# Decoder trunk on one core: FFN openings of four columns side by side, and x issued from ScalarE's queue

## The chip, the cores and the metric

The kernel runs on one core of a Trainium2 chip. The metric is the device time of one execution in microseconds (us); the time of a kernel is the median of several executions.

## The reference

Two layers work on a residual `h` of 256 positions by 1024 features in float32. Each layer has an FFN, a mixer and a second FFN; layer 0's mixer is attention (two head groups), layer 1's a Mamba-2 block.

```
for layer in range(2):
    h = h + 0.5 * swiglu(rmsnorm(h, ffn1_norm[layer]), w_gate, w_up, w_down)
    h = h + mixer(rmsnorm(h, mix_norm[layer]))
    h = h + 0.5 * swiglu(rmsnorm(h, ffn2_norm[layer]), w_gate, w_up, w_down)

swiglu(x) = (silu(x @ w_gate) * (x @ w_up)) @ w_down     # 1024 -> 2816 -> 1024
rmsnorm(x, g) = x * rsqrt(mean(x * x) + eps) * g
```

So there are four FFNs. The change concerns how each of them begins, and how the first one gets its data.

## The kernel before, in words

**Layout.** `h` lies transposed in SBUF: 8 tiles (`KT` = 8, index k) of 128 features by 256 positions. All products are made from split operands: a float32 number is cut into a high part and a low rest, and a product is high x high + high x low + low x high. `refresh(k)` (lines 202 to 210) makes the two halves of input tile k: ScalarE scales `h` by the gain into the high half of `xhl` (L205), VectorE computes the low half (L206). `squares(k)` (L212 to L216) squares `h` on ScalarE (L214) and adds up on POOL into `sqa` (L216).

**Weights.** All weights stream through class `Weights` in the order of use, as units of 128 x 1024 numbers (512 KB). SyncE's queue loads a unit into one of 4 `raw` buffers (L71); ScalarE rounds it to the high part `hi` (L86, a cast), VectorE subtracts for the low part `lo` (L87), into one of 8 pairs of buffers. `take()` (L91) hands out a unit and queues the conversion of units up to 4 ahead. The first unit is converted in four parts of 256 columns, the second in two of 512, all others whole.

**An FFN.** `ffn` (L356) makes 22 gate columns and 22 up columns of 128 outputs each (index f), then 8 down columns. A column is 8 *pieces*, one for each k; a piece (L338) is two matmuls, L339 (`hi` against both halves of the input, 512 wide) and L340 (`lo` against the high half, 256 wide). Both halves of a sum land in one PSUM bank. `total` (L360) copies the right half out on ScalarE (L363) and adds it on VectorE (L365). `gate` multiplies by the norm factor `rB` (L370), applies Silu (L371) and multiplies again (L372); `up` multiplies the two sums (L377) and splits the result into `ht` (L184, L185). In the first f the gate column and the up column run up to k = 6, and both get their k = 7 after that.

**The norm.** The norm factor of a row isn't put into the input: it is multiplied onto the sums afterwards. So the matmuls of a stage can begin before the norm is known. `norm_job` (L218) is a job in two steps among the matmuls: step one sums `sqa` over partitions on TensorE (L223), VectorE adds eps (L227), POOL takes the power -1/2 (L228); step two spreads the result over partitions on TensorE (L233) and ScalarE copies it to SBUF as `rB` (L237).

**What sets the order.** Each piece advances a clock of the program by 0.35 (`tick`, L341); a posted job makes its next step when the clock passes its due time. `post_norm` (L241) posts the norm with a delay of `L_N0` = 6.5, and its second step comes `L_N1` = 3.0 later. `need(nj)` (L384) makes whatever steps are left at once; it stands at the end of f = 0, after 16 pieces. A scheduler then orders each engine's instructions; `high_priority` moves instructions forward. Within an engine, instructions run in that order.

**The start of the program.** SyncE issues the gains `gn`, then parts of the input x and of weight unit 0 in turn (L130, L136), then the next units. TensorE has six matmuls on an identity matrix as a warm-up (L855; each of these float32 matmuls shows as two in the profile). `refresh` runs for k = 0 to 7 with the conversions of three units between, and then the squares.

PSUM has 8 banks: four in pool `mm` (`bank()`), two in `sb` (`sbank()`, used by the mixers alone) and two in `tp` (`tbank()`).

## Time and profile before

| | |
|---|---|
| median of 3 runs | 1083.4 us (1081.33 to 1087.55) |
| the profiled execution | 1074.93 us, its span 1073.1 us |
| TensorE busy | 1043.1 us, 97% of the span |
| VectorE busy | 808.7 us, 75% |
| ScalarE busy | 621.0 us, 58% |
| POOL busy | 99.4 us, 9% |
| mean granted clock of TensorE | 0.993 of full |
| read from HBM | 189.12 MB, 177 GB/s over the span |

PE is TensorE's matmul stream and PEld its weight loads, DVE is VectorE, ACT is ScalarE, SP is SyncE. A row of the timeline gives start, duration, engine, line, operation, output and inputs, shapes and the number of instructions in the row; in brackets the idle time before it and what ended it. Matmuls overlap their neighbours, so the pace of a stream is read from starts, not from durations. The profiled execution is about 8 us shorter than the median of the runs; sums are made against its rows.

### The profile page before, as it was taken

What the parts mean: (1) busy time and instruction counts of PE and PEld (TensorE: products, weight loads), DVE (VectorE), ACT (ScalarE), POOL (GpSimd) and SP (SyncE); (2) the same over time, 40 slices, a digit from 0 to 9 for tenths busy, and PEclk for the clock granted to TensorE, in tenths of its full rate; (3) what the DMA queues carried; (4) which work ended last, traced back from release to release, by engine and by line L of the source; (5) the groups of instructions that cost most, each with busy time, mean ns of one, the idle gap of its engine ahead of it and who ended that gap; (6) DMA issues with size and microseconds to landing.
All of it is one profiled execution on the core that took longest, in us unless ns stands there. A gap on an engine that the chain in (4) does not pass through costs nothing.

```text
span 1073.1 us, 17287 instructions
## 1 busy us (share of the span) xinstructions
PE 1043.1 (97%) x6538; PEld 919.3 (86%) x6538; DVE 808.7 (75%) x1261; ACT 621.0 (58%) x1099; POOL 99.4 (9%) x117
## 2 busy tenths in 40 slices
PE   6999999997999999999999999999899999999998
PEld 5888888885888888888888888998888998888887
DVE  4898876666788888766888876587889768888751
ACT  5765654555666555454655654478878656555530
POOL 3000001243020000011000001101231121000000
PEclk8999999999999999999999999999999999999999
DMA  6776565534237666665666666534565636666550
GB/s 216 227 238 195 185 190 194 179 138 139 97 94 225 193 191 185 193 193 168 198 189 195 186 189 194 188 107 157 181 223 188 218 118 202 191 197 183 190 177 20
DMA packets 61603, 191.33 MB, mean 178 GB/s; under 512 B 6440, under 2 KB 15952, under 8 KB 61392
## 3 DMA queue, kind: packets, MB, share of 16 engines
q1 hardware_dynamic: 61520, 190.23, 56.5%
q8 instruction: 51, 0.84, 0.3%
q14 instruction: 32, 0.26, 0.1%
HBM read 189.12 MB, written 1.09 MB: 177 GB/s over the span
## 4 chain that ended last, share of the span: by engine, by line
PE 81%; DVE 5%; POOL 4%; ACT 3%; issue 3%; DMA 3%; SPq 0%; POOLq 0%; DVEq 0%; ACTq 0%
PE mm L339 44%; PE mm L340 23%; PE mm L258 3%; PE mm L260 3%; PE mm L259 3%; DMA seg<-scr_a 1%; DVE lo L87 1%; POOL rstd L194 1%; PE mm L253 1%; PE mm L254 1%; PE mm L255 1%; POOL sqa L216 1%; DVE cv L704 1%; ACT hi L86 1%; PE sb L767 1%
## 5 line engine op out<-in xcount | busy, mean ns | idle before, releaser
L86 ACT CAST hi<-raw 128x1024 fp32r<-128x1024 f32 (+1 forms) x350 | 362.6, 1041 | 346.9 <-PE mm L339 274.1
L87 DVE TENSOR_TENSOR lo<-raw,hi 128x1024 fp32r<-128x1024 f32 (+1 forms) x350 | 426.3, 1222 | 146.2 <-ACT hi L86 145.0
L339 PE MATMUL mm<-xhl,hi 128*128 128x512 f32 x1408 | 494.1, 395 | 7.2 <-ACT hi L86 4.9
L340 PE MATMUL mm<-xhl,lo 128*128 128x256 f32 x1408 | 395.9, 281 | 0.0
L339 PEld LDWEIGHTS mm<-xhl,hi 128*128 128x128 f32 x1408 | 265.6, 189 | 67.0 <-ACT hi L86 4.8
L340 PEld LDWEIGHTS mm<-xhl,lo 128*128 128x128 f32 x1408 | 268.3, 191 | 0.3 <-DVE lo L87 0.2
L339 PE MATMUL mm<-ht,hi 128*128 128x512 f32 x704 | 244.2, 392 | 0.0
L340 PE MATMUL mm<-ht,lo 128*128 128x256 f32 x704 | 197.0, 280 | 0.0
L339 PEld LDWEIGHTS mm<-ht,hi 128*128 128x128 f32 x704 | 131.8, 187 | 29.1
L340 PEld LDWEIGHTS mm<-ht,lo 128*128 128x128 f32 x704 | 133.2, 189 | 0.0
L216 POOL TENSOR_TENSOR sqa<-sqa,sqb 128x256 f32<-128x256 f32 x42 | 38.7, 921 | 597.0 <-ACT sqb L214 595.9
L253 PE MATMUL mm<-hi,xhl 128*128 128x512 f32 (+1 forms) x144 | 58.6, 407 | 0.0
L258 PE MATMUL mm<-xhl,hi 128*128 128x256 f32 x192 | 56.5, 294 | 0.0
L254 PE MATMUL mm<-lo,xhl 128*128 128x512 f32 (+1 forms) x144 | 55.5, 386 | 0.0
L255 PE MATMUL mm<-hi,xhl 128*128 128x512 f32 (+1 forms) x144 | 55.1, 383 | 0.0
L259 PE MATMUL mm<-xhl,hi 128*128 128x256 f32 x192 | 54.9, 286 | 0.0
L260 PE MATMUL mm<-xhl,lo 128*128 128x256 f32 x192 | 54.8, 285 | 0.0
L407 DVE SCALAR_TENSOR_TENSOR h<-mm,h 128x256 f32<-128x256 f32 x64 | 26.6, 422 | 36.5 <-PE mm L340 35.8
L206 DVE SCALAR_TENSOR_TENSOR xhl<-h,gn,xhl 128x256 fp32r<-128x256 f32 x48 | 35.8, 768 | 8.2 <-ACT xhl L205 8.2
L370 DVE TENSOR_TENSOR sumg<-sumg,rB 128x256 f32<-128x256 f32 x88 | 37.4, 425 | 4.9 <-ACT rB L237 2.3
L372 DVE TENSOR_TENSOR sumg<-sumg,rB 128x256 f32<-128x256 f32 x88 | 36.9, 419 | 4.4 <-ACT sumg L371 4.4
L377 DVE TENSOR_TENSOR sumu<-sumu,sumg 128x256 f32<-128x256 f32 x88 | 37.4, 425 | 2.6
(192 smaller groups left out, 1246.0 us busy)
## 6 DMA issues: line engine op xcount, KB each, us to landing
raw<-in_wp_dram SPq DMA_DIRECT2D x345, 512.0 KB, 3.6
seg<-scr_a SPq DMA_DIRECT2D x8, 512.0 KB, 7.0
fbc<-scr_f SPq DMA_DIRECT2D x1, 1024.0 KB, 5.7
ng<-in_ssm_norm_dram SPq DMA_DIRECT2D x4, 256.0 KB, 3.6
out_dram<-h SPq DMA_DIRECT2D x8, 128.0 KB, 2.7
h<-in_x_dram SPq DMA_DIRECT2D x3, 256.0 KB, 6.2
raw<-in_wp_dram SPq DMA_DIRECT2D x2, 256.0 KB, 2.7
smt<-in_sm_dram SPq DMA_DIRECT2D x1, 319.5 KB, 4.1
```

The source lines that it names most:

```text
L86: self.nc.scalar.copy(hi[:, cs], w[:, cs])
L87: self.nc.vector.tensor_tensor(lo[:, cs], w[:, cs], hi[:, cs].bitcast(F32), ALU.subtract)
L216: G.tensor_tensor(sqa, sqa, q, ALU.add)
L253: T.matmul(acc, sh, wh, start=start, stop=False)
L254: T.matmul(acc, sh, wl, start=False, stop=False)
L255: T.matmul(acc, sl_, wh, start=False, stop=stop)
L258: T.matmul(acc, wh, mh, start=start, stop=False)
L259: T.matmul(acc, wh, ml, start=False, stop=False)
L260: T.matmul(acc, wl, mh, start=False, stop=stop)
L339: T.matmul(acc, wh, mhl.rearrange("p e c -> p (e c)"), start=start, stop=False)
L340: T.matmul(acc[:, 0:S], wl, mhl[:, 0, :], start=False, stop=stop)
L370: V.tensor_tensor(s_, s_, rn[1], ALU.mult)
```

## The change

Three things are changed.

1. **FFN opening.** Each of the four FFNs opens with two gate and two up columns side by side: for k = 0 to 5, one piece of each of the four columns, then k = 6 and 7 column by column (`START`). The four sums take two banks of `sb` and two of `mm`; the next columns find the other two `mm` banks, so six banks are in use. The weights of these four columns are packed in this order, one unit for two k's.
2. **The first norm later.** The sums of the opening are brought to SBUF by `total` and kept there (`bufs=4`); columns of later f's join them in the list `late`. From f = `ready` on (4 in the first FFN, 3 in the others), each f finishes two of the waiting ones (Silu, products, `ht`) until none is left. In the first FFN the norm is posted with a delay of 16.5 and without priority; in the others the delay of 6.5 stays, but nothing makes its steps come early any more, since `need` stands at f = 3.
3. **The start.** x and the gains are issued from ScalarE's queue, the weights from SyncE's; units 1 to 3 are issued at once. The warm-up matmuls work on a zeroed tile and stand at the very beginning of TensorE's order. The conversions of the first four units are interleaved with the refreshes.

```
+START = [(b, k) for k in range(KT - 2) for b in range(4)]
+START += [(b, k) for b in range(4) for k in range(KT - 2, KT)]
...
-    nc.sync.dma_start(gn, gains)
+    nc.scalar.dma_start(gn, gains)
     W.load(1)
-    for a in ((h[:, 0:1, :], x[:, 0:1, :]), (W.raws[0][:, 0:512], wp[0, :, 0:512]),
...
-        nc.sync.dma_start(*a)
+    for c0, c1 in ((0, 256), (256, 1024)):
+        nc.sync.dma_start(W.raws[0][:, c0:c1], wp[0, :, c0:c1])
+    for k0, k1 in ((0, 1), (1, 2), (2, 4), (4, 6), (6, 8)):
+        nc.scalar.dma_start(h[:, k0:k1, :], x[:, k0:k1, :])
+    W.load(RAW)
+    idle = cp.tile([P, P], F32, name="idle")
+    V.memset(idle, 0.0)
+    warm = tbank()
+    for _ in range(WARM):
+        T.matmul(warm[:, 0:P], idle, idle, start=True, stop=True)
...
+            accs = [sbank(), sbank(), bank(), bank()]
+            us = [W.take()]
+            for n, (b, k) in enumerate(START):
+                if n and n % 8 == 0:
+                    us.append(W.take())
+                ks = slice(n % 8 * P, (n % 8 + 1) * P)
+                piece(accs[b], us[-1][0][:, ks], us[-1][1][:, ks], xhl[:, k], k == 0, k == KT - 1)
+                if n % 8 == 7:
+                    W.free()
+                if k == KT - 1:
+                    accs[b] = total(accs[b], "gu"[b % 2])
+            late = [(0, accs[0], accs[1]), (1, accs[2], accs[3])]
+            def finish():
+                q, a, b = late.pop(0)
+                gate(a)
+                up(q, b, a)
-            for f in range(NFT):
+            for f in range(2, NFT):
                 g_, u_ = bank(), bank()
+                column(g_)
+                if f == ready:
+                    need(nj)
+                if f >= ready and late:
+                    finish()
+                s_ = total(g_, "g")
+                ahead = not late
+                if ahead:
+                    gate(s_)
+                column(u_)
+                t_ = total(u_, "u")
+                if ahead:
+                    up(f, t_, s_)
                 else:
+                    late.append((f, s_, t_))
+                    if f >= ready:
+                        finish()
...
     for k in range(KT):
         last = refresh(k, 0, False)
-        if k in (1, 5, 7):
-            W.ahead((1, 5, 7).index(k) + 1)
+        if k % 2 == 0:
+            first = W.convert()
+        next(first, None)
+    W.ahead(RAW + 1)
     with tc.issue_after(last.ins):
         for k in range(KT):
             squares(k)
-    nj = post_norm()
-    nj = ffn(nj, 1)
+    nj = post_norm(L_NX, 0)
+    nj = ffn(nj, 1, 4)
```

**The order at three places.** Lines of the changed kernel have other numbers: the pieces are L356 and L357 there, refresh L222 and L223, squares L231, casts L92 and L93, the sums L375 and L377, the norm's rows L240, L244 (VectorE), L245 (POOL) and L250.

The first place is the start of ScalarE's order. Before:

```order
L144 ACT_TABLE_LOAD
L144 ACTIVATE one_97<-one_97 128x2
L205 ACTIVATE xhl<-h,gn 128x256
L86 CAST hi<-raw 128x256 x2
L205 ACTIVATE xhl<-h,gn 128x256 x3
L86 CAST hi<-raw 128x256 x2
L205 ACTIVATE xhl<-h,gn 128x256 x4
L214 ACTIVATE sqa<-h 128x256
L214 ACTIVATE sqb<-h 128x256 x2
```

In the change (`gn` and `h` are the gains and x on their way in; L161 is the first table load):

```order
L141 DMA gn<-in_gains_dram 128x48
L146 DMA h<-in_x_dram 128x256 x2
L146 DMA h<-in_x_dram 128x512 x3
L161 ACT_TABLE_LOAD
L161 ACTIVATE one_112<-one_112 128x2
L222 ACTIVATE xhl<-h,gn 128x256
L92 CAST hi<-raw 128x256 x2
L222 ACTIVATE xhl<-h,gn 128x256
L92 CAST hi<-raw 128x256 x2
L222 ACTIVATE xhl<-h,gn 128x256
L92 CAST hi<-raw 128x512
```

Six DMA issues stand ahead of the table load and of every refresh, and the casts of the first units stand between the refreshes.

The second place is VectorE's order around the first norm (`rn<-tp`), in the first FFN. Before:

```order
L206 SCALAR_TENSOR_TENSOR xhl<-h,gn,xhl 128x256 x4
L87 TENSOR_TENSOR lo<-raw,hi 128x512 x2
L87 TENSOR_TENSOR lo<-raw,hi 128x1024
L227 TENSOR_SCALAR rn<-tp 128x2
L87 TENSOR_TENSOR lo<-raw,hi 128x1024
L365 TENSOR_TENSOR sumg<-mm,log 128x256
L87 TENSOR_TENSOR lo<-raw,hi 128x1024
L370 TENSOR_TENSOR sumg<-sumg,rB 128x256
```

In the change:

```order
L223 SCALAR_TENSOR_TENSOR xhl<-h,gn,xhl 128x256
L93 TENSOR_TENSOR lo<-raw,hi 128x1024 x4
L377 TENSOR_TENSOR sumg<-sb,log 128x256
L377 TENSOR_TENSOR sumu<-sb,lou 128x256
L377 TENSOR_TENSOR sumg<-mm,log 128x256
L377 TENSOR_TENSOR sumu<-mm,lou 128x256
L93 TENSOR_TENSOR lo<-raw,hi 128x1024
L377 TENSOR_TENSOR sumg<-mm,log 128x256
L93 TENSOR_TENSOR lo<-raw,hi 128x1024
L244 TENSOR_SCALAR rn<-tp 128x2
L377 TENSOR_TENSOR sumu<-mm,lou 128x256
```

The norm's row now stands behind the sums of the four opening columns and behind the `lo` parts of seven more units (ten are ahead of it, three were).

The third place is TensorE's order in the opening of the second FFN, from the first step of the norm (`tp<-one`) to its second (`tp<-ident,rn`). Before, with 16 pieces of the FFN ahead of these rows:

```order
L340 MATMUL mm<-xhl,lo 128x256
L223 MATMUL tp<-one_97,sqa 64x2 x4
L339 MATMUL mm<-xhl,hi 128x512
L340 MATMUL mm<-xhl,lo 128x256
L339 MATMUL mm<-xhl,hi 128x512
L340 MATMUL mm<-xhl,lo 128x256
L339 MATMUL mm<-xhl,hi 128x512
L233 MATMUL tp<-ident,rn 128x128 x2
L340 MATMUL mm<-xhl,lo 128x256
```

In the change 19 pieces stand ahead of the first step and 9 between the two; the rows around the first and around the second are

```order
L356 MATMUL mm<-xhl,hi 128x512
L357 MATMUL mm<-xhl,lo 128x256
L240 MATMUL tp<-one_112,sqa 64x2 x4
L356 MATMUL mm<-xhl,hi 128x512
L357 MATMUL mm<-xhl,lo 128x256
```

```order
L356 MATMUL sb<-xhl,hi 128x512
L357 MATMUL sb<-xhl,lo 128x256
L356 MATMUL sb<-xhl,hi 128x512
L357 MATMUL sb<-xhl,lo 128x256
L250 MATMUL tp<-ident,rn 128x128 x2
L356 MATMUL mm<-xhl,hi 128x512
L357 MATMUL mm<-xhl,lo 128x256
```

The first step has moved back by three pieces here, by three in the third FFN and by seven in the last; between the steps there were 3, 2 and 4 pieces and are now 9 in each.

## Rows read from the trace of the kernel before

**Rows 1.** The page: busy time of each engine, share of the span, instructions.

```profile
PE 1043.1 (97%) x6538; PEld 919.3 (86%) x6538; DVE 808.7 (75%) x1261; ACT 621.0 (58%) x1099; POOL 99.4 (9%) x117
```

**Rows 2.** Waits of TensorE: total us, times, longest us.

```profile
PE tp L223 <- POOL sqa L216: 3.2, 2, 2.0
PE tp L233 <- POOL rn L228: 2.9, 4, 1.3
```

**Rows 3.** Timeline of TensorE, the opening: start us, us, instruction, [idle before].

```profile
4.87 0.76 PE L339 MATMUL mm<-xhl,hi 128*128 128x512 f32 x1 [4.87 <-ACT hi L86]
...
19.47 0.40 PE L223 MATMUL tp<-one,sqa 128*64 128x2 f32 x8 [1.97 <-POOL sqa L216]
...
21.85 1.23 PE L233 MATMUL tp<-ident,rn 128*128 128x128 f32 x4 [1.31 <-POOL rn L228]
...
23.51 0.63 PE L339 MATMUL mm<-xhl,hi 128*128 128x512 f32 x1
...
24.15 0.63 PE L339 MATMUL mm<-xhl,hi 128*128 128x512 f32 x1
...
38.45 0.39 PE L339 MATMUL mm<-xhl,hi 128*128 128x512 f32 x1
```

**Rows 4.** Stretches: us, busy (and count) of PE, PEld, DVE, ACT, POOL; granted clock.

```profile
20.50:27.20 6.70, 5.39 (x19) 4.68 (x19) 3.85 (x5) 1.84 (x4) 1.29 (x1) 0.50 0.59 164
...
38.45:138.45 100.00, 100.00 (x579) 88.30 (x578) 86.86 (x150) 61.64 (x112) 0.00 (x0) 1.00 0.67 212
```

**Rows 5.** Timeline of ScalarE, the opening.

```profile
0.72 1.28 ACT L144 ACT_TABLE_LOAD   x1 [0.72 <-PEq L956]
2.01 0.20 ACT L144 ACTIVATE one<-one 128x2 f32<-128x2 f32 x1
3.70 0.51 ACT L205 ACTIVATE xhl<-h,gn 128x256 fp32r<-128x256 f32 x1 [1.48 <-DMA h<-in_x_dram]
...
7.95 0.69 ACT L86 CAST hi<-raw 128x256 fp32r<-128x256 f32 x2
9.73 1.71 ACT L205 ACTIVATE xhl<-h,gn 128x256 fp32r<-128x256 f32 x4 [1.08 <-DMA h<-in_x_dram]
...
11.64 0.71 ACT L214 ACTIVATE sqb<-h 128x256 f32<-128x256 f32 x2
...
17.04 0.42 ACT L214 ACTIVATE sqb<-h 128x256 f32<-128x256 f32 x1 [1.26 <-POOL sqa L216]
...
28.96 1.98 ACT L86 CAST hi<-raw 128x1024 fp32r<-128x1024 f32 x2
```

**Rows 6.** Timelines of VectorE and of POOL, the opening.

```profile
21.14 0.42 DVE L365 TENSOR_TENSOR sumg<-mm,log 128x256 f32<-128x256 f32 x1
21.48 1.21 DVE L87 TENSOR_TENSOR lo<-raw,hi 128x1024 fp32r<-128x1024 f32 x1
...
12.13 7.29 POOL L216 TENSOR_TENSOR sqa<-sqa,sqb 128x256 f32<-128x256 f32 x7 [10.84 <-ACT sqb L214]
20.16 1.64 POOL L228 TENSOR_TENSOR rn<-rn,mhalf 128x2 f32<-128x2 f32 x1 [0.74 <-DVE rn L227]
```

**Rows 7.** Timeline of SyncE, the opening: issues of x.

```profile
1.17 0.42 SPq L136 DMA_DIRECT2D h<-in_x_dram  x1
...
3.53 0.91 SPq L136 DMA_DIRECT2D h<-in_x_dram  x2
```

**Rows 8.** Timeline of TensorE, the openings of the three later FFNs.

```profile
317.44 0.51 PE L339 MATMUL mm<-xhl,hi 128*128 128x512 f32 x1 [0.86 <-DVE xhl L206]
...
322.89 0.49 PE L233 MATMUL tp<-ident,rn 128*128 128x128 f32 x2 [0.90 <-POOL rn L228]
...
507.10 0.49 PE L233 MATMUL tp<-ident,rn 128*128 128x128 f32 x2 [0.27 <-POOL rn L228]
...
888.24 0.40 PE L223 MATMUL tp<-one,sqa 128*64 128x2 f32 x8 [1.26 <-POOL sqa L216]
...
890.68 0.49 PE L233 MATMUL tp<-ident,rn 128*128 128x128 f32 x2 [0.44 <-POOL rn L228]
```

More of the change, by code (lines that the diff above doesn't have):

```diff
@@ L341, in piece, with column, ffn @@
         tick(0.35)
-    def columns(runs):
-        us = {}
-        for q, acc, k0, k1 in runs:
-            if q not in us:
-                us[q] = W.take()
-            wh, wl = us[q]
-            for k in range(k0, k1):
-                ks = slice(k * P, (k + 1) * P)
-                piece(acc, wh[:, ks], wl[:, ks], xhl[:, k], k == 0, k == KT - 1)
-            if k1 == KT:
-                W.free()
-    def ffn(nj, norm):
+    def column(acc):
+        wh, wl = W.take()
+        for k in range(KT):
+            ks = slice(k * P, (k + 1) * P)
+            piece(acc, wh[:, ks], wl[:, ks], xhl[:, k], k == 0, k == KT - 1)
+        W.free()
+    def ffn(nj, norm, ready=3):
         with tc.tile_pool(name="ffp", bufs=1, reuse_waits="tile") as fp:
@@ L849, in ssm @@
                             lambda k: yhl[k // 4][1][:, k % 4, :], norm, before)
-    warm = tbank()
-    for _ in range(WARM):
-        T.matmul(warm[:, 0:P], ident, ident, start=True, stop=True)
     for k in range(KT):
         last = refresh(k, 0, False)
-        if k in (1, 5, 7):
-            W.ahead((1, 5, 7).index(k) + 1)
+        if k % 2 == 0:
+            first = W.convert()
+        next(first, None)
+    W.ahead(RAW + 1)
     with tc.issue_after(last.ins):
```

69 lines of the change are left out of this document (33 added, 36 removed).

## The prediction

> **What bounds the kernel now.** I read the page's busy times first. TensorE is busy for 1043.1 of 1073.1 us [rows 1]: the program is one stream of matmuls, and only what interrupts or slows that stream can be won. VectorE, at 75%, is next.
>
> Then the waits of TensorE. Those that belong to the beginning of a stage are that of the norm's first step for POOL's sum of squares (3.2 us) and of its second step for the power on POOL (2.9 us) [rows 2]. Before the first piece there are 4.87 us more [rows 3].
>
> Then the timeline, to see where they lie. In the first FFN the norm's steps stop TensorE for 1.97 and 1.31 us [rows 3], and behind them the granted clock is 0.50, the 1.2 GHz level, from 20.5 to 27.2 us [rows 4]. Pieces then start 0.64 us apart (23.51, 24.15) [rows 3]. At full clock 579 matmuls take 100 us [rows 4], so a piece, which is two of them, takes 0.346 us. The 58th piece starts at 38.45 us [rows 3]; 57 pieces at full clock are 19.7 us, so 18.7 us of the first 38.45 are start, waits and slow clock. In the other FFNs the waits are 0.86 us for refreshed input and 0.90 for the norm (second FFN), 0.27 us (third), 1.26 and 0.44 us (last) [rows 8].
>
> **The change, part by part.**
>
> *Number of instructions.* Pieces, conversions, sums and products stay the same in number, and the order of the mixers is untouched. Only the four openings count. I measure the first by the moment at which TensorE has 57 pieces and both steps of the norm behind it: 38.45 us now; in the change the second step stands behind 48 + 9 = 57 pieces.
>
> *The issues on ScalarE.* Six issues now stand ahead of its table load. On SyncE two take 0.91 us [rows 7]; ScalarE shows none. Bounds: nothing, or SyncE's price, 6 x 0.455 = 2.7 us. I take 2.7, the only row there is for the same operation. Then the table load of 1.28 us and the small activation of 0.20 us [rows 5]: the first refresh starts at 0.72 + 2.7 + 1.3 + 0.2 = 4.9 us, where it is at 3.70 now [rows 5]. So the start itself is 1.2 us later. The table load is priced by its row: the instruction behind it starts at 2.01, 1.29 us after the load [rows 5]. The Trainium skill (ScalarE: Activation LUTs, What ACT_TABLE_LOAD costs) gives a switch 1.28 us plus a drain of 1.38 us; by that the first refresh would be at 6.3 us and the gain below 1.4 us smaller, but this trace has no room for the drain.
>
> *ScalarE up to the sums.* From there its order is fixed: eight refreshes, four casts of 256 columns, two of 512, three of 1024, two squares' starts. Rows of one kind overlap a little, so I take starts: (1.71 - 0.51)/3 = 0.40 a refresh, about 0.33 for a cast of 256 (0.69 a pair), 0.94 for a whole one (1.98 a pair) [rows 5], and 0.54 for one of 512, between the two. That is 3.2 + 1.3 + 1.1 + 2.8 + 0.35 = 8.8 us, and the first `sqb` starts at 13.7. From the first `sqb` to the end of the last square it is 11.64 to 17.46 now, 5.8 us, because POOL's seven additions take 7.29 us and ScalarE waits for a free buffer [rows 5, 6]; I keep the 5.8: 19.5 us. Only then come the casts of units 5, 6 and 7 (2.8 us): 22.3 us.
>
> *VectorE up to the norm.* It takes the low part of unit 7 (1.21 us [rows 6]): 23.5; the four sums, 0.34 each from start to start (21.14 to 21.48 [rows 6]): 24.9; two more units (1.2 each) and one sum: 27.6; the norm's row, about 0.15; then POOL's power, 1.64 us [rows 6]: 29.4 us. The second step on TensorE may then start; it takes about 0.5 us at full clock (the two rows of 0.49 [rows 8] are a half each, overlapping). That makes 29.9 us.
>
> *TensorE up to there.* First piece at 4.9 + 0.5 (ScalarE) + 0.5 (VectorE) = 5.9 us. It has no work between its warm-up, done by about 4 us, and that, so I price 8 pieces at 0.64, as behind the stops now, and 40 at 0.346: 24.9 us. POOL's sum is done by 13.7 + 0.4 + 7.3 = 21.4, so the first step doesn't wait. With 0.4 for it and 9 pieces more it is 28.4 us. So a wait of 1.0 us remains at the second step, and ScalarE, POOL and VectorE set the end of this stage, not TensorE.
>
> *Landing of x and weights.* The x parts issued from 3.53 were refreshed at 9.73, 6.2 us later [rows 7, 5]. With that delay unit 1, issued at about 1.6, lands at 7.8 instead of the 7.4 at which ScalarE wants it. If all transfers issued in the first 3.4 us slow each other further, I bound it by 9.7. The price is 0 to 2.3 us; I take 0.5, since these transfers are issued a microsecond or two earlier than now and the units behind them not at once. So 30.4 us against 38.45: **8.0 us**.
>
> *The other three openings.* Between the first step and the second there are 9 pieces (3.1 us) instead of 2 to 4; in the second FFN POOL's power lay within 2.1 us of the first step. In the last FFN the first step comes seven pieces (2.4 us) later, which covers its 1.26. Input tile 6 is wanted after 24 pieces instead of 6, which covers the 0.86. So all of 0.86 + 0.90 + 0.27 + 1.26 + 0.44 = **3.7 us** goes. What is late next is a PSUM bank: f = 2 finds two free ones, but f = 3 takes the bank of the third opening column. In the first FFN its sum is read by 23.5 + 3 x 0.34 = 24.5 us, and piece 49 wants it at 25.3; in the others the squares are done long before, so the margin is larger.
>
> *The sums kept.* At f = 3 to 5 (4 to 6 in the first FFN) VectorE finishes two f's in one: four more operations of 0.42 us [rows 6]. It is busy for 86.86 of 100 us in such a stretch [rows 4], an idle 0.73 us in the 5.54 us of an f. So it falls behind by 1 us an f, 3 us in all. This costs nothing, as the conversions run ahead: by the sum above unit 10 has its low part at about 30 us and its first piece comes at 38. Without that lead it would cost what the last rival says.
>
> *Sum.* 8.0 + 3.7 = 11.7 us: the profiled execution would go from 1074.9 to 1063.2. The median of the runs is 8.5 us above that execution, and I take the same off it: 1083.4 - 11.7 = **1071.7 us**.
>
> **The rivals.**
>
> *The start is bound by transfers.* All 3.3 MB that are wanted first share the engines, x arrives no sooner than now, and ScalarE, POOL and VectorE move back by 2.3 us; with issues on ScalarE some tenths dearer than on SyncE the opening wins 5 us. For it: 6.2 us from issue to use [rows 7, 5]. Against: the first x was used 2.5 us after its issue at 1.17 [rows 7, 5]. It gives 1083.4 - 5 - 3.7 = 1074.7 us. The Trainium skill (DMA: Bandwidth & Descriptors, Issuing engines are not separate DMA queues) says that a second issuing queue saves only issue time; by that rule this rival is what the move of x to ScalarE comes to, and no row here has two queues at work.
>
> *The wait for the norm comes back.* The second step in the first FFN waits 3 us instead of 1, because VectorE's norm row stands behind two conversions, and the clock falls behind it as it does now [rows 3, 4]: 7 pieces at 0.29 more are 2.0. The opening then wins 8 - 4 = 4 us, the others perhaps 1. That is 1078.4 us, no change by the measure below. For it: the norm's place in VectorE's order. Against: in the last FFN's opening 1.26 us did not bring the clock down: the second step there has two matmuls in 0.49 us [rows 8], where at 21.85 four took 1.23 [rows 3].
>
> *VectorE becomes the bound (slower).* If the lead of the conversions is under 3 us when the double finishing begins, TensorE waits for `lo`: 1 us in three f's of four FFNs, 11.4 us, and in each FFN the clock falls for 7 pieces, 2.0 us more: 19.4 - 11.7 = 7.7 us slower, 1091.1 us. For it: 87% busy [rows 4]. Against: the opening takes these very operations off VectorE before, and the lead computed above is 8 us.
>
> **How the numbers follow.** Forecast 0.65, transfers 0.16, norm 0.13, VectorE 0.06. A measurement of this kernel can tell about 0.5%, 5.4 us, from no change. Forecast and first rival lie beyond that, the second rival within it: faster 0.80, same 0.14, slower 0.06. For the range: free issues on ScalarE give 1.2 us more, waits that restart without loss about 1, and the runs of before differ from their median by up to 4 us; the low end is 1064. The high end, 1079, takes in both middle rivals. Only the last, and tails, lie outside.
>
> **What would show it.** In the profile after: the first refresh near 4.9 us and the first piece near 5.9; about 8 pieces 0.64 apart; the second norm step behind 57 pieces near 30 us, with about 1 us of waiting for POOL; no waits over 0.3 us in the other three openings; TensorE's span shorter by 11 to 12 us, and its busy time lower by some 3 us of slow pieces. I am wrong if x is refreshed with long waits for transfers, if pieces at f = 3 to 7 wait for `lo`, or if new waits for banks stand at the seventh column.

## The result, and the profile after

| | median of the runs | the runs | profiled execution: span |
|---|---|---|---|
| before | 1084.56 us | 1081.33 to 1087.55 (4) | 1073.1 us (its time 1074.93) |
| the change | 1071.3 us | 1070.77 to 1075.17 (4) | 1073.3 us (its time 1075.17) |

The ratio is 0.9884, with an interval of 0.9852 to 0.9915: the change is faster by 13.3 us, 1.2%. The forecast was 1071.7 us, a gain of 11.7 on the median of 1083.4 that before had then. Yet the two *profiled* spans are equal, and TensorE is busy for 1051.4 us, not the 1043.1 of [rows 1]. So either the openings did not win what was forecast, or something else took it back. The page of the change:

```profile
PE 1051.4 (98%) x6538; PEld 920.5 (86%) x6538; DVE 806.0 (75%) x1262; ACT 621.3 (58%) x1099; POOL 98.6 (9%) x117
```

**The start.** Timeline of ScalarE, the first 9 us of the change (start, duration, engine, line, operation; ACTq rows are issues; in brackets the idle time before and what ended it); it answers to [rows 5]:

```profile
0.72 0.40 ACTq L141 DMA_DIRECT2D gn<-in_gains_dram  x1
1.16 2.55 ACTq L146 DMA_DIRECT2D h<-in_x_dram  x5
3.73 1.28 ACT L161 ACT_TABLE_LOAD   x1 [3.73 <-DMA gn<-in_gains_dram]
5.03 0.20 ACT L161 ACTIVATE one<-one 128x2 f32<-128x2 f32 x1
5.58 0.51 ACT L222 ACTIVATE xhl<-h,gn 128x256 fp32r<-128x256 f32 x1 [0.35 <-DMA h<-in_x_dram]
...
7.86 0.51 ACT L222 ACTIVATE xhl<-h,gn 128x256 fp32r<-128x256 f32 x1 [1.17 <-DMA h<-in_x_dram]
```

The six issues take 3.0 us, from 0.72 to 3.73, and the table load stands behind them. The first refresh then still waits 0.35 us for x, the second 1.17: the first part of x is used 4.4 us after its issue at 1.16, where it was 2.5 us before [rows 7, 5]. The view of the DMA issues (queue, number, size, median us from issue to landing) says the same of the first two parts of x, before and in the change:

```profile
h<-in_x_dram SPq DMA_DIRECT2D x2, 128.0 KB, 2.5
```

```profile
h<-in_x_dram ACTq DMA_DIRECT2D x2, 128.0 KB, 5.3
```

The three parts of 256 KB land 8.4 us after their issue, 6.2 before.

**The norm.** Timeline of VectorE, the change, around the norm's row:

```profile
28.22 1.21 DVE L93 TENSOR_TENSOR lo<-raw,hi 128x1024 fp32r<-128x1024 f32 x1
29.35 0.15 DVE L244 TENSOR_SCALAR rn<-tp 128x2 f32<-128x2 f32 x1
```

Timeline of POOL, the same stretch of the change:

```profile
16.35 6.93 POOL L233 TENSOR_TENSOR sqa<-sqa,sqb 128x256 f32<-128x256 f32 x7 [15.06 <-ACT sqb L231]
29.58 0.71 POOL L245 TENSOR_TENSOR rn<-rn,mhalf 128x2 f32<-128x2 f32 x1 [6.29 <-DVE rn L244]
```

Timeline of TensorE, the change, the norm's two steps and the 58th piece (30.81); it answers to [rows 3]:

```profile
26.32 0.40 PE L240 MATMUL tp<-one,sqa 128*64 128x2 f32 x8
...
30.34 0.71 PE L250 MATMUL tp<-ident,rn 128*128 128x128 f32 x4 [0.26 <-POOL rn L245]
30.81 0.48 PE L356 MATMUL mm<-xhl,hi 128*128 128x512 f32 x1
```

Step one no longer waits, step two waits 0.26 us, and the 58th piece starts at 30.81 us, where it was at 38.45. So the opening did what was forecast. To the 100th piece, where all after-effects are past, it is 45.72 us instead of 53.01: 7.3 us. The start of that piece, before and in the change:

```profile
53.01 0.39 PE L339 MATMUL mm<-xhl,hi 128*128 128x512 f32 x1
```

```profile
45.72 0.40 PE L356 MATMUL mm<-xhl,hi 128*128 128x512 f32 x1
```

Counted from an FFN's first piece to its 100th, the others take 35.94, 35.48 and 36.45 us, where they took 37.70, 35.84 and 37.85: 3.5 us more. So 10.8 us are won in the openings, and lost elsewhere in this one execution.

**Where they were lost.** Busy time of TensorE in 80 us of each FFN, behind its opening: the stretch, its length, busy time, in brackets the number of matmuls, the granted clock, DMA share, GB/s. Before:

```profile
50.00:130.00 80.00, 80.00 (x464) 1.00 0.67 213
330.00:410.00 80.00, 80.00 (x463) 1.00 0.64 195
530.00:610.00 80.00, 80.00 (x464) 1.00 0.61 191
910.00:990.00 80.00, 80.00 (x464) 1.00 0.61 189
```

The change:

```profile
50.00:130.00 80.00, 80.00 (x455) 1.00 0.66 202
330.00:410.00 80.00, 80.00 (x454) 1.00 0.63 191
530.00:610.00 80.00, 80.00 (x464) 1.00 0.61 190
910.00:990.00 80.00, 80.00 (x455) 1.00 0.60 187
```

The same matmuls at the same granted clock of 1.00 (2.4 GHz), without a wait, and in three of four FFNs nine fewer of them in 80 us. From start to start a piece takes 346.7 ns in the one kind and 353.3 ns in the other. The pace that the norm's second step leaves stays to the end of the FFN: some 1000 matmuls, each 80/455 - 80/464 us = 3.4 ns longer, make **3.4 us an FFN**. Part of that lies ahead of the 100th piece already; from the 100th piece to the last, a slow FFN takes 151.23 us and a fast one 148.37, so three slow ones lose 8.6 us. Another 2.4 us are lost in the stretch between the third FFN's last piece and the last FFN's first piece, whose code is the same: 197.9 us in the first profile of before and 200.3 in this one; over all profiles it takes 197.9 to 200.5 us in no order that follows the kernels. Together that is 11.0 us, as much as the openings had won.

In the second and the last FFN the norm's second step does not make the slow pace, though. In all ten profiles of kernels with four columns (this one and those below), these two run at 353.6 ns a piece from their first piece to the norm, whatever follows. Between the norm's two steps it is the slow pace too, in all but two of their openings, and even where the FFN was fast up to step one, as the first FFN is here. So what the second step does is to end the slow pace or to leave it.

So there are two questions: which part of the change wins the openings, and whether the slow pace belongs to the change or to the execution.

### The profile page after: what moved, and what is told of

The parts are those of the page before. It is cut to its first block, busy times and chain, and to the rows that moved or that the text cites. A ratio compares the mean times of both kernels' runs of the same rounds, so it can differ in the third digit from the quotient of the medians.

```text
span 1073.3 us, 17290 instructions
## 1 busy us (share of the span) xinstructions
PE 1051.4 (98%) x6538; PEld 920.5 (86%) x6538; DVE 806.0 (75%) x1262; ACT 621.3 (58%) x1099; POOL 98.6 (9%) x117
## 4 chain that ended last, share of the span: by engine, by line
PE 82%; DVE 4%; DMA 4%; POOL 3%; issue 3%; ACT 3%; SPq 0%; POOLq 0%; ACTq 0%; DVEq 0%
PE mm L356 43%; PE mm L357 22%; PE mm L275 3%; PE mm L277 3%; PE mm L276 3%; DMA seg<-scr_a 1%; DVE lo L93 1%; PE mm L270 1%; POOL rstd L211 1%; PE mm L271 1%; PE mm L272 1%; DMA raw<-in_wp_dram 1%; DVE cv L742 1%; ACT hi L92 1%; POOL sqa L233 1%
## 5 line engine op out<-in xcount | busy, mean ns | idle before, releaser
L92 ACT CAST hi<-raw 128x1024 fp32r<-128x1024 f32 (+1 forms) x350 | 362.0, 1040 | 357.4 <-PE mm L356 274.4
L93 DVE TENSOR_TENSOR lo<-raw,hi 128x1024 fp32r<-128x1024 f32 (+1 forms) x350 | 424.9, 1219 | 160.9 <-ACT hi L92 159.3
L356 PE MATMUL mm<-xhl,hi 128*128 128x512 f32 x1344 | 475.8, 398 | 0.0
L357 PE MATMUL mm<-xhl,lo 128*128 128x256 f32 x1344 | 377.6, 281 | 0.0
L356 PEld LDWEIGHTS mm<-xhl,hi 128*128 128x128 f32 x1344 | 252.8, 188 | 60.9
L357 PEld LDWEIGHTS mm<-xhl,lo 128*128 128x128 f32 x1344 | 254.5, 189 | 0.0
L356 PE MATMUL mm<-ht,hi 128*128 128x512 f32 x704 | 247.8, 397 | 0.0
L357 PE MATMUL mm<-ht,lo 128*128 128x256 f32 x704 | 197.6, 281 | 0.0
L356 PEld LDWEIGHTS mm<-ht,hi 128*128 128x128 f32 x704 | 132.1, 188 | 32.0
L357 PEld LDWEIGHTS mm<-ht,lo 128*128 128x128 f32 x704 | 133.0, 189 | 0.0
L277 PE MATMUL mm<-xhl,lo 128*128 128x256 f32 x192 | 55.3, 288 | 0.0
L223 DVE SCALAR_TENSOR_TENSOR xhl<-h,gn,xhl 128x256 fp32r<-128x256 f32 x48 | 36.0, 767 | 8.4 <-ACT xhl L222 8.4
L381 DVE TENSOR_TENSOR sumg<-sumg,rB 128x256 f32<-128x256 f32 x88 | 37.3, 424 | 2.3
L275 PEld LDWEIGHTS mm<-xhl,hi 128*128 128x128 f32 x192 | 37.8, 197 | 0.7 <-issue 0.5
```

The source lines that it names most:

```text
L92: self.nc.scalar.copy(hi[:, cs], w[:, cs])
L93: self.nc.vector.tensor_tensor(lo[:, cs], w[:, cs], hi[:, cs].bitcast(F32), ALU.subtract)
L275: T.matmul(acc, wh, mh, start=start, stop=False)
L277: T.matmul(acc, wl, mh, start=False, stop=stop)
L356: T.matmul(acc, wh, mhl.rearrange("p e c -> p (e c)"), start=start, stop=False)
L357: T.matmul(acc[:, 0:S], wl, mhl[:, 0, :], start=False, stop=stop)
```

## The experiments

What an edit does to the first opening is read from the start of the first FFN's 58th or 100th piece, since the pace blurs the whole time.

### The parts of the change, with both kernels beside them

Before, once more:

> The kernel before once more, in the same call as the three below, for its trace. What is in question: in the first profile of it, all four FFNs take 346.7 ns a piece (two matmuls) at full granted clock after their norm; in the first profile of the change, three of the four take 353.3 ns, some 500 pieces each, 3.4 us an FFN. Theory P (the pace is a thing of its own, drawn anew in each execution): this profile has another number of slow FFNs than none, and its span is 1073.1 + 3.4 us for each of them. Theory Q (the pace belongs to the code): again none slow, span 1073.1 within 0.5. By both the 58th piece starts at 38.4 and the norm stops TensorE for 2.0 and 1.3 us in the first FFN.

Measured: a median of 1079.11 us, 1075.55 to 1083.58 (other runs of before at the same time: 1080.06, 1077.71 to 1083.31). Again no FFN is slow, and the span is 1074.7, not 1073.1: 1.3 of the 1.6 us lie in the stretch ahead of the last FFN named above. So theory P's other pattern did not come, and Q's span neither; this run alone settles nothing.

The start alone, put into the kernel before (the FFNs keep `columns` and its order):

```
-    nc.sync.dma_start(gn, gains)
+    nc.scalar.dma_start(gn, gains)
...
+    for k0, k1 in ((0, 1), (1, 2), (2, 4), (4, 6), (6, 8)):
+        nc.scalar.dma_start(h[:, k0:k1, :], x[:, k0:k1, :])
+    W.load(RAW)
...
+        if k % 2 == 0:
+            first = W.convert()
+        next(first, None)
```

> The kernel before with the change's start alone (x and gains issued on ScalarE, the early warm-up, conversions between the refreshes); the FFNs open as before, with one gate and one up column. Theory A (the four opening columns and the late norm bring the gain): the first piece starts later than before, at 6.5 to 7 us as in the change, because of the issues ahead of ScalarE's table load; the norm stops TensorE again by 2 to 4 us in all, pieces at 1.2 GHz follow, and the 58th piece starts at 38 to 40 us, against 38.4 before and 30.8 in the change. The later FFNs don't change. Time within 2 us of before, apart from the pace of the FFNs. Theory B (the start brings half or more): the 58th piece at 34.5 us or sooner and 4 us or more off the time.

Waits of TensorE up to 30 us (engine, line waited for: us, times, longest), and its 58th piece:

```profile
PE tp L237 <- POOL sqa L230: 3.1, 1, 3.1
...
PE tp L247 <- POOL rn L242: 0.8, 1, 0.8
```

```profile
38.26 0.39 PE L353 MATMUL mm<-xhl,hi 128*128 128x512 f32 x1
```

Theory A holds: first piece at 6.62, 3.9 us of waits for the norm, 58th piece at 38.26 where before has 38.45; the ratio is 1.0012 [0.9995, 1.0029]. By itself the start is worth nothing. Eight more pieces stand ahead of the norm's first step than in before, but that step comes 2.9 us later too (22.38 instead of 19.47), since it waits for POOL's sum, and the slow clock follows as before (0.62 granted from 25 to 31 us).

The opening alone, that is the change with its start taken back:

```
-    nc.scalar.dma_start(gn, gains)
+    nc.sync.dma_start(gn, gains)
...
-        if k % 2 == 0:
-            first = W.convert()
-        next(first, None)
+        if k in (1, 5, 7):
+            W.ahead((1, 5, 7).index(k) + 1)
```

> The change without its start: x issued on SyncE behind and between the first weights, warm-up and whole conversions as before; four opening columns, kept sums and the late norm stay. Theory A: first piece at 4.9 us as before, the squares end by 17.5 and the norm is not later than in the change, so the 58th piece starts between 30 and 33 us; all of the 3.7 to 4.6 us of the later openings is won. Time within 2 us of the change's and 9 to 12 below before, apart from the pace. Theory B: without the interleaved conversions the units come too late for four columns' first pieces (unit 1 behind six refreshes), TensorE waits 4 us or more for them, and the 58th piece is at 35 us or later.

Its 58th piece:

```profile
32.31 0.48 PE L342 MATMUL mm<-xhl,hi 128*128 128x512 f32 x1
```

Theory A again: 32.31 lies in its 30 to 33, and the ratio is 0.9912 [0.9881, 0.9943], 1070.1 us beside 1069.56 of the change. Four columns with the late norm carry 6 of the 7.6 us in the first FFN and everything in the others; with them there, the start is worth the remaining 1.4 us (32.31 to 30.90; how exact that is, the run with a later step two shows below).

The change, once more:

> The change once more beside before on the same chip. Opening as in its first profile: first piece at 6.8, second norm step at about 30.3 without a wait over 0.3 us, 58th piece at 30.8. Theory P (pace drawn anew in each execution): the four FFNs show another pattern of 346.7 and 353.3 ns than slow, slow, fast, slow, and the span is about 1063 us + 3.4 for each slow one. Theory Q (the pace belongs to the code): the same pattern and a span of 1073.3 within 0.5, and the four columns cost 10 us that the openings pay for.

Measured: 1069.56 us, 1067.16 to 1072.15; ratio 0.9899 [0.9873, 0.9925]. The 58th piece is at 30.90, and the 100th at 45.56 where the profile of before taken beside it has 53.14. The matmuls in 80 us:

```profile
50.00:130.00 80.00, 80.00 (x463) 1.00 0.69 206
330.00:410.00 80.00, 80.00 (x455) 1.00 0.61 191
530.00:610.00 80.00, 80.00 (x464) 1.00 0.62 191
910.00:990.00 80.00, 80.00 (x463) 1.00 0.63 191
```

The same program, and now only the second FFN is slow: span 1066.4 = 1063 + 3.4. So in the first and the last FFN the pace differs from execution to execution, as theory P says. The second was slow in both.

### The late norm, the queue of x, the warm-up, the place of step two

The norm of the first FFN back at its old place, in the change:

```
-    nj = post_norm(L_NX, 0)
-    nj = ffn(nj, 1, 4)
+    nj = post_norm()
+    nj = ffn(nj, 1)
```

With that, `need` stands at f = 3 again instead of 4.

> The change, but with the first FFN's norm at the old place (step one after 19 pieces, its row and power with the old priority, needed at f = 3). Theory A (the late norm is what the four columns need in the first FFN): the 19th piece ends near 16.5 us, POOL's sum of squares is there only at 23, so the norm's first step stops TensorE for 5 to 7 us, pieces at 1.2 GHz follow, and the 58th piece starts at 34 to 36 us instead of 30.8; 3.5 to 5 us slower than the change. Rival: the units' conversions bound the opening anyway and the wait only moves, 58th piece at 31.5 or sooner, time as the change within 1 us.

Waits of TensorE up to 40 us, and the 58th piece:

```profile
PE tp L240 <- POOL sqa L233: 3.3, 1, 3.3
...
PE tp L250 <- POOL rn L245: 1.2, 1, 1.2
```

```profile
35.92 0.39 PE L356 MATMUL mm<-xhl,hi 128*128 128x512 f32 x1
```

The first step waits 3.3 us, less than the 5 to 7 expected, as it came to stand behind 30 pieces and not 19. With the second step's wait it is 4.5 us; the clock falls behind it (0.76 granted from 23 to 30 us), and the 58th piece is 5.0 us late, as theory A said. The 100th is at 50.48. Time 1076.99, ratio 0.9961 [0.9929, 0.9992]: most of the change's gain is gone. The late norm is needed. The late norm with one gate and one up column, without the four, was not run.

x and gains back on SyncE, in the change:

```
+    nc.sync.dma_start(gn, gains)
...
+    for q in ((h[:, 0:1, :], x[:, 0:1, :]), (W.raws[0][:, 0:256], wp[0, :, 0:256]),
+              (h[:, 1:2, :], x[:, 1:2, :]), (W.raws[0][:, 256:], wp[0, :, 256:]),
+              (h[:, 2:4, :], x[:, 2:4, :]), (h[:, 4:6, :], x[:, 4:6, :]),
+              (h[:, 6:8, :], x[:, 6:8, :])):
+        nc.sync.dma_start(*q)
```

> The change, but gains and x issued on SyncE as before, between the two halves of the first weight unit, and units 1 to 3 behind them. Theory A (six issues ahead of ScalarE's table load cost 2.7 us and x loses another 1.9 us by sharing transfers with units 1 to 3): first refresh at 4.0 to 4.5 us instead of 5.6, first piece at 5.0 to 5.6 instead of 6.7; but the norm's row stands behind VectorE's conversions, whose units 2 to 7 come no sooner, so the 58th piece moves by 0.3 to 1.2 us only, to 29.6 to 30.4; time 0 to 1 us below the change, less than the runs can tell. Rival (two queues are what makes the start): the last parts of x are issued at 4 us and later and land after 10 us, TensorE waits for them, 58th piece at 31.5 us or later.

Here theory A was wrong and the rival right. The first piece comes at 4.83 us, 1.9 us sooner and earlier still than it said, but then the parts run out. ScalarE's wait for the second part of unit 0 (issued fifth, at 2.57), and the 58th piece:

```profile
6.80 1.02 ACT L92 CAST hi<-raw 128x256 fp32r<-128x256 f32 x3 [1.49 <-DMA raw<-in_wp_dram]
```

```profile
32.28 0.48 PE L357 MATMUL mm<-xhl,hi 128*128 128x512 f32 x1
```

TensorE waits 2.6 us for weights and x, and its pieces still go 0.64 us apart at 16 us; in the two profiles of the change they do so to 12.65 and to 9.4 us. So the 16th piece is at 16.78 us (14.79 and 13.36 in the change) and the 58th at 32.28, 1.4 to 1.5 us later. That is the same as in the opening alone, which also issues x on SyncE: so the queue of x is what the start's gain comes from, and six issues ahead of ScalarE's table load cost less than they save on SyncE. The time is 1074.26 us, ratio 0.9923 [0.9896, 0.9951], with two slow FFNs in its profile.

A longer warm-up, in the change:

```
-WARM = 6
+WARM = 13
```

> The change with 13 warm-up matmuls instead of 6, so that TensorE has work until about 6.7 us, when the first piece can start. Theory A: the clock rises at about 7 us instead of 12.6, nine pieces take 0.35 instead of 0.64 us, and TensorE is at the norm's first step 2.6 us sooner; but POOL's sum is there only at 23.4 and the norm's row on VectorE only at 29.4, so step two waits 2 to 3 us more instead, and behind it the clock falls for up to 8 pieces: 58th piece at 30.5 to 31, time the same or up to 2 us slower than the change. Rival (TensorE itself bounds the opening, and the row moves up with it): 58th piece at 28.2, time 2.6 us below the change.

The end is as theory A says (58th piece 30.61, 100th 45.52; the change 30.90 and 45.56), the way not: TensorE does reach its 32nd piece sooner (18.40, 19.01), but gives it back in three waits of 0.4 to 0.7 us, and step two waits 0.34, not 2 to 3 us more. What is late is VectorE, for it has nothing to do while ScalarE squares: four of ScalarE's squares wait 0.4 to 0.65 us each for a buffer that POOL has yet to read, and the casts that VectorE needs stand behind them. The timeline of VectorE in this kernel:

```profile
21.19 4.11 DVE L93 TENSOR_TENSOR lo<-raw,hi 128x1024 fp32r<-128x1024 f32 x3 [4.47 <-ACT hi L92]
```

The median is 1074.26 us (0.993 [0.9901, 0.9959]), with three slow FFNs in its profile: the pace hides what an opening does.

Step two of the second FFN two pieces later, in the change (the third norm of the program is that FFN's):

```
+LATER = {3: 3.7}
...
-        yield L_N1
+        jobs_seen[0] += 1
+        yield LATER.get(jobs_seen[0], L_N1)
```

> The change with one edit: in the second FFN alone the norm's second step stands two pieces later (11 behind the first step, not 9). The slow pace repeats itself every three pieces (gaps over the columns of 23, 6, 19, 11, 28, 13 ns at the six matmuls), and in all three profiles of four-column openings the second FFN's step two fell behind the third of these pieces and left the pace slow, in the third FFN behind the second of them and left it fast. Theory P (the place in this cycle at which the norm interrupts sets the pace that follows): two pieces later is the place of the third FFN, the second FFN then takes 346.7 ns a piece, 3.3 us less than the change's 353.3. Rival 1 (the slow pace of the second FFN belongs to the opening or the tiles): it stays at 353.3. Rival 2 (chance): either, and other FFNs change too.

The second FFN stays slow (455 matmuls in 80 us; time 1072.56 us, 0.9909 [0.9876, 0.9943]), so theory P in this form is wrong: the place in the three-piece cycle does not decide by itself.

This kernel's first FFN has the change's code, and its 58th piece is at 31.35 us and its 100th at 46.27. So one and the same opening differs by 0.5 to 0.7 us between executions, and the 1.4 us of the start above are known no better than 0.7 to 1.6.

### A better opening, and the place between two matmuls

```
-WARM = 6
+WARM = 13
+LATER = {1: 6.65, 3: 3.3, 6: 3.3}
...
-        q = cp.tile([P, S], F32, tag="sq", name="sqb", bufs=3) if k else sqa
+        q = cp.tile([P, S], F32, tag="sq", name="sqb", bufs=7) if k else sqa
...
         T.matmul(acc, wh, mhl.rearrange("p e c -> p (e c)"), start=start, stop=False)
+        tick(0.175)
         T.matmul(acc[:, 0:S], wl, mhl[:, 0, :], start=False, stop=stop)
-        tick(0.35)
+        tick(0.175)
```

> The change with three edits. (1) 13 warm-up matmuls; (2) seven buffers for the squares instead of three, so that ScalarE does not wait for POOL's additions with the casts of units 5 to 7 behind them; (3) the first FFN's second norm step 19.5 pieces behind the first instead of 9, in the second and the last FFN 9.5 pieces, so that step two stands between the two matmuls of a piece there. Theory A for the opening (after the longer warm-up what is late is VectorE's idle 4.5 us before the low part of unit 5, which waits for ScalarE's squares): the squares end at about 18 instead of 20.2, the norm's row comes 2 us sooner, no wait of TensorE over 0.4 us behind the 16th piece, and the 58th piece starts at 27 to 28 us instead of 30.6 to 30.9; 2.5 to 3.5 us off the time. Rival: transfers bound it (weights for units 4 to 7), 58th piece at 30 or later. Theory for the pace: in before's second and third FFN, where step two stood between the two matmuls of a piece, the pace behind it was the fast one in 6 of 6; if that place is what does it, the second and the last FFN take 346.7 ns here, 3.3 us less in the second than any four-column kernel so far. Rival: the second stays at 353.3, as in 7 of 7 profiles with four columns.

The same with step two behind whole pieces (19, 10 and 10), without the half ticks:

```
+LATER = {1: 6.5, 3: 3.4, 6: 3.4}
```

> As the kernel beside it in the opening, but with step two behind whole pieces: 19 pieces in the first FFN, 10 (not 9 or 11) in the second and the last. Opening: 58th piece at 27 to 28 us by theory A, at 30 or later by the rival. Pace: if the place between two matmuls is what makes it fast, the second FFN stays at 353.3 ns a piece here and this kernel is 3.3 us (one FFN) to 6.6 us (two) slower than the one beside it; if the number of pieces decides, 10 is the one of three places in the cycle that has not been tried, and the second FFN may be fast here too; by chance alone, each FFN draws for itself.

Opening: ScalarE's squares now stand together, VectorE idles 2.17 instead of 4.47 us, and the norm's row comes at 27.80 instead of 29.15 with the longer warm-up alone (29.35 in the change). Timelines of ScalarE, VectorE and POOL in the first of the two:

```profile
16.11 2.24 ACT L233 ACTIVATE sqb<-h 128x256 f32<-128x256 f32 x7
```

```profile
19.33 4.58 DVE L94 TENSOR_TENSOR lo<-raw,hi 128x1024 fp32r<-128x1024 f32 x3 [2.17 <-ACT hi L93]
...
27.80 0.15 DVE L246 TENSOR_SCALAR rn<-tp 128x2 f32<-128x2 f32 x1
```

```profile
16.59 8.73 POOL L235 TENSOR_TENSOR sqa<-sqa,sqb 128x256 f32<-128x256 f32 x7 [15.30 <-ACT sqb L233]
```

The 58th piece is at 29.06 and 28.84 us, between theory A's 27 to 28 and the rival's 30; but here step two stands behind 67 pieces, so the 58th does not have its 0.5 us behind it, as it has in the change. The 100th is the fair mark: 44.08 and 44.13, some 1.5 us ahead of the change, where 2.5 to 3.5 were expected. Some of it went back: VectorE's conversions now run beside POOL's seven additions, which take 8.73 us instead of 6.93, and step one waits 0.4 and 0.5 us for them.

Pace: matmuls in 80 us, step two between the two matmuls of a piece (not in the third FFN):

```profile
50.00:130.00 80.00, 80.00 (x464) 1.00 0.71 210
330.00:410.00 80.00, 80.00 (x463) 1.00 0.64 197
530.00:610.00 80.00, 80.00 (x463) 1.00 0.62 191
910.00:990.00 80.00, 80.00 (x464) 1.00 0.64 191
```

and behind whole pieces:

```profile
50.00:130.00 80.00, 80.00 (x455) 1.00 0.69 207
330.00:410.00 80.00, 80.00 (x454) 1.00 0.64 194
530.00:610.00 80.00, 80.00 (x455) 1.00 0.62 186
910.00:990.00 80.00, 80.00 (x463) 1.00 0.65 190
```

Times: **1062.65 us** (1061.61 to 1065.35; ratio 0.9846 [0.9822, 0.987]) and 1073.04 (1070.28 to 1074.3; 0.9934 [0.9914, 0.9954]). With openings within 0.05 us of each other at the 100th piece, ten microseconds lie between them, three FFNs' worth. The first is the best kernel of this study: its median is 7 to 9 us below the change's, but these were measured at other times, and by the ratios to before (0.9846 beside 0.9884 and 0.9899) it is 4 to 6 us.

### The place alone, in the change and in before

In the change, the half ticks and a later step two, so that it stands between the two matmuls of a piece in all four FFNs; warm-up and buffers untouched:

```
+LATER = {3: 3.3, 4: 3.3, 6: 3.3}
```

> The change with one thing altered: the norm's second step stands between the two matmuls of a piece in all four FFNs (9 pieces behind step one in the first, 9.5 in the others); warm-up and buffers as in the change. Up to now every step two between the two matmuls of a piece left the fast pace (10 of 10), one behind a whole piece in 19 of 38. Theory (the place sets the pace): all four FFNs take 346.7 ns a piece, the opening is the change's (58th piece at 30.6 to 31.2), the span is 1063 to 1064 us, the time 1064.5 to 1066 and the runs within 3 us of each other: 5 to 7 us below the change's median, and 1.5 to 3 above the kernel with the longer warm-up and more buffers. Rival (in that kernel the opening or chance made the pace): one or more FFNs at 353.3 again, second FFN first, and the time is the change's 1069 to 1071.

In before, for the last FFN alone, the norm is called for between the two matmuls of its 16th piece, where step two then comes to stand four pieces on:

```
+    mid = []
...
+        if mid and stop:
+            g = mid.pop()
+            if g is not None:
+                need(g)
...
+                    if norm is None:
+                        mid.extend([nj, None])
```

> The kernel before with one thing altered: in the last FFN the norm's second step stands between the two matmuls of the 20th piece (as it does in the second and third FFN of before already), not behind it. In the first FFN it stays behind a piece. Theory (the place sets the pace, and the 8 to 13 us between the runs of before are FFNs that fell into the slow one): the last FFN is fast in every run, runs above 1081 us are gone or rare, the median is 1 to 2 us below before's, and the time of an undisturbed run stays at 1075. Rival (before's spread has another cause): median and spread as before's.

The change with step two between: 1068.67 us (1066.37 to 1071.07; 0.9882 [0.9853, 0.9911]), not the 1064.5 to 1066 of the theory and no better than the change's own ratios; the 58th piece is at 31.36. Its matmuls in 80 us of the second and the third FFN:

```profile
330.00:410.00 80.00, 80.00 (x464) 1.00 0.63 197
530.00:610.00 80.00, 80.00 (x455) 1.00 0.61 187
```

The second FFN is fast, for the first time with four columns but for the better opening above; but the third is slow, although its step two stands between two matmuls. So "the place sets the pace" is too strong. Before with that edit: 1079.82 us (1075.81 to 1088.14), ratio 0.9991 [0.9964, 1.0017], its last FFN fast and its first slow: inconclusive, and its widest runs remain, against the theory.

All profiles together; s marks a slow FFN, and a letter in brackets one whose step two stands between the two matmuls of a piece; the last column is the span less 3.4 us for each slow FFN:

| kernel | FFN 1, 2, 3, 4 | span | at one pace |
|---|---|---|---|
| before, first profile | f (f) (f) f | 1073.1 | 1073.1 |
| before, again | f (f) (f) f | 1074.7 | 1074.7 |
| before, last norm between | s (f) (f) (f) | 1076.3 | 1072.9 |
| start alone | f (f) (f) s | 1078.7 | 1075.3 |
| norm early | (f) s f s | 1075.2 | 1068.4 |
| opening alone | f s f f | 1067.7 | 1064.3 |
| x on SyncE | s s f f | 1071.0 | 1064.2 |
| **the change**, first profile | s s f s | 1073.3 | 1063.1 |
| **the change**, again | f s f f | 1066.4 | 1063.0 |
| 13 warm-up matmuls | s s f s | 1072.7 | 1062.5 |
| step two later | s s f s | 1073.0 | 1062.8 |
| the change, norms between | (f) (f) (s) (f) | 1066.0 | 1062.6 |
| better opening, whole pieces | s s s f | 1070.2 | 1060.0 |
| better opening, between | (f) (f) f (f) | 1060.8 | 1060.8 |

At one pace the kernels fall in the order that their openings give: before and the start alone at 1073 to 1075, the early norm at 1068, the change and its neighbours at 1062.5 to 1064, the better opening at 1060 to 1061. Of 17 steps two between two matmuls one left the slow pace, of 39 behind a whole piece 20. These are not independent draws: behind whole pieces with four columns the second FFN was slow 8 times of 8, the third once in 9, while the first and the last came out either way in the very same program.

## Why the prediction was right

**The bound and the parts.** The openings were forecast to win 8.0 us in the first FFN and 3.7 in the others. Measured to the 100th piece they won 7.3 (53.01 to 45.72) and, in the second pair of profiles, 7.6 (53.14 to 45.56); in the others 3.5, and 4.0 where the last FFN is fast. Sum 10.8 to 11.6, forecast 11.7; at one pace the spans differ by 10 to 11.7 us.

**The chain in the first FFN, step by step.** Errors of one to two microseconds cancelled:
- *Issues on ScalarE*: 3.0 us, forecast 2.7; the table load's 1.28 and the next activation right behind it as forecast. The drain of 1.38 us that the Trainium skill gives (ScalarE: Activation LUTs, What ACT_TABLE_LOAD costs) is again not seen: load at 3.73, next activation at 5.03.
- *First refresh* 5.58 for 4.9, first piece 6.76 for 5.9. The term for transfers was mis-sized: ScalarE waits 0.35 and 1.17 us for x and 0.28 for a weight unit, 1.8 us for the forecast's 0.5. x itself comes later (4.4 us instead of 2.5 after its issue), as the first rival held, and not unit 1. (What that rival wants first, x, four units and the gains, is 3.2 MB and not 3.3.) So the first `sqb` starts at 15.87 us, forecast 13.7, and of the sign "x is refreshed with long waits for transfers" there is one, of 1.17 us. That these 2.2 us do not show at the end is due to the squares and POOL's power, which were priced 1.25 and 0.93 us too high.
- *Slow pieces* at the start: nine 0.64 us apart, to 12.65 us, forecast 8.
- *Squares* 4.55 us (15.87 to 20.42), forecast 5.8; *VectorE's norm row* at 29.35, forecast 27.6. One low part lasts 1.76 us instead of 1.21 beside POOL's last addition, which itself takes 1.61 us where most take 0.74. Timelines of VectorE and of POOL, the change:

```profile
22.61 1.76 DVE L93 TENSOR_TENSOR lo<-raw,hi 128x1024 fp32r<-128x1024 f32 x1
```

```profile
21.68 1.61 POOL L233 TENSOR_TENSOR sqa<-sqa,sqb 128x256 f32<-128x256 f32 x1
```

The Trainium skill (SBUF — State Buffer, Who interferes with whom) says that a VectorE instruction with two SBUF inputs contends with a GpSimd instruction that reads SBUF; the 1.76 and 1.61 us, and POOL's 8.73 instead of 6.93 us in the better opening, agree with it.
- *POOL's power* 0.71 us, forecast 1.64. The 1.64 was read where a low part ran beside it (VectorE from 20.00 to 21.23 us, POOL from 20.16); in the change the power starts at 29.58, behind the low part that ends at 29.43.
- *Step two* at 30.34 with a wait of 0.26, forecast 29.4 with 1.0; 58th piece 30.81, forecast 30.4.

**The later openings.** As forecast: the waits of [rows 8] are gone but for 0.2 to 0.3 us at the last FFN's step two.

**The sums kept.** No wait of TensorE for a low part anywhere in the profile after, and one of 0.3 us in the change's second profile: the rival of VectorE as the bound fell. The bank that the forecast named as next to be late is so by 0.7 us in the second profile of the change and not at all in the first.

**The other rivals.** The wait for the norm comes back only if the norm stays early: 35.92 instead of 30.9. Of x on ScalarE the first rival said that it saves issue time alone. With x on SyncE the parts of x land sooner after their issue (2.5 and 5.5 us, where it is 5.3 and 8.4 in the change), but unit 0's second part is issued at 2.57 us and not by 1.59, and the opening is 0.9 to 1.6 us slower. So this issue time is worth something once four columns want x and three units at once.

**What was wrong.** "TensorE's span shorter by 11 to 12 us, and its busy time lower by some 3" did not come true in the profile after: span equal, busy time 8.3 us higher. The step that failed is that pieces cost the same in both kernels, "579 matmuls take 100 us" [rows 4], so that the sum has no term for a change of pace. There are two paces, 346.7 and 353.3 ns a piece or 3.4 us an FFN, and the first profile of before had four fast FFNs out of four. That execution, 1074.93 us, lies below nearly all runs of before (1074.29 to 1088.61 over all experiments, medians 1079.1 to 1084.6). The forecast took the 8.5 us between it and the median along as a constant. It held because the change's medians too lie above what one pace would give (1063 us of span and 1.9 around it), by 5 to 6 us; that these are slow FFNs is what the profiles suggest, but unprofiled runs show no pace, so this part stays argued. What lifts the median of before above its profiled executions is not known: two of its profiles have no slow FFN at all. With the other medians of before the same working would have given 1067 to 1073 us: the gain is right to 1 or 2 us, the agreement within 0.4 us is luck.

## What to carry to other kernels

Put other work between a reduction and its use, enough columns to cover the slowest engine's chain, and move the reduction's place with it: here the faster start alone won nothing, and four columns with the norm at its old place kept some 2.7 of the 7.6 us. Read a gain at a mark in the program (the 58th piece, the 100th) and count the matmuls in equal stretches before comparing spans; a pace that differs by 2% is invisible in waits and in the granted clock and hid all of a 1% gain in one profile. When one engine idles in an opening, look for the buffer count that makes its supplier wait: three buffers instead of seven cost VectorE 2.3 us of idling here and the norm's row 1.4 us.

## What the hardware showed that was not expected

**Two paces of TensorE.** At granted clock 1.00 the same stream of matmuls ran at 464 or at 455 matmuls in 80 us, and kept its pace for some 500 pieces, until the next norm or the mixers. In the trace the slow pace repeats every three pieces, with 23, 6, 19, 11, 28 and 13 ns over the columns' time at the six matmuls, 16.7 ns in the mean; the fast one has 13.3. In these profiles the pace changed only where something interrupts the stream, at the norm's small matmuls above all; an FFN of the four-column kernels that comes behind a mixer began at the slow pace each time. The Trainium skill (TensorE: Matmul & The Clock Gate, Back-to-back issue gap) gives 2.5 ns over the columns at the 2.4 GHz level for a matmul by itself, and says that a stream of weight loads and matmuls is spaced by both. The stream here, with a weight load for each matmul, has more than 2.5 ns in either pace. Step two between the two matmuls of a piece went with the fast pace 16 times of 17, and of two kernels whose openings agree to 0.05 us the one with step two there was 10 us faster, but the cause is not settled: neither the place in the cycle nor this place decides by itself, and nothing tried here shows what does.

**The clock after the same waits.** In before the norm's two stops (1.97 and 1.31 us) were followed by a granted clock of 0.50 from 20.5 to 27.2 us [rows 3, 4], and in its second profile (1.85 and 1.31 us) by 0.51 in the same stretch. In before with the last norm moved, the first FFN is unchanged and stopped for 1.83 and 1.31 us, yet the clock stayed at 1.00. The stretches of TensorE and the other engines, this kernel (the columns PE, PEld, DVE, ACT, POOL, then the granted clock):

```profile
20.50:27.20 6.70, 6.20 (x36) 5.46 (x37) 4.03 (x7) 4.90 (x8) 0.45 (x1) 1.00 0.71 201
```

36 matmuls instead of 19, and the 100th piece at 50.16 us instead of 53.01: 3 of the 7.3 us that the change wins in the first FFN were there in one profiled execution of before's first FFN already. How often that happens, the unprofiled runs do not show.
